# Weight chunks with the hi parts together and the lo parts behind them, at new places modulo 256 bytes

## The chip, the cores and the metric

The kernel runs on one NeuronCore of one Trainium2 chip. The metric is the device time of one execution in microseconds, the median of several runs. The profile is of one further execution.

## The reference, cut to what matters

The reference is a decoder trunk of two layers on 256 tokens of 2048 channels, in float32. Layer 0 mixes tokens with stick-breaking attention (8 heads) and a Mamba-2 SSD beside it; layer 1 with a mixture of dilated attentions (16 heads). Each layer ends with a gated ConvFFN of width 5632. Nearly all arithmetic is in large products of the activations with weight matrices:

```python
proj = hn @ w_in                      # even: 2048 x 5648, odd: 2048 x 6144
h = h + (o @ w_out)                   # 2048 x 2048 in both layers
g = causal_dwconv(hn @ w_gate, conv_w, conv_b)      # 2048 x 5632
f = (jax.nn.silu(g) * (hn @ w_up)) @ w_down         # 5632 x 2048
```

## The kernel before

Activations are kept transposed, channels on partitions and the 256 tokens along the free dimension. Each float32 operand of a large product is split into two float32r parts, hi and lo, and hi\*hi, lo\*hi and hi\*lo are summed in PSUM. An activation tile is 512 columns wide: hi parts of 256 tokens, then lo parts. Its name tells the stage: `x` holds the normed input of a layer or FFN, `act` the gated FFN activations, `o` the mixers' outputs.

A weight matrix is read in panels of 256 output channels and in chunks of `CH` = 4 tiles of 128 input channels. `prep` (lines 110 to 128) gets one chunk: a DMA brings 512 KB to `raw` (four buffers), ScalarE copies it to float32r as the hi parts (line 126), and VectorE subtracts these from `raw` for the lo parts (line 127). Both go to one tile `hl` of three buffers, in which each of the four tiles has its 256 hi columns and behind them its 256 lo columns.

`chan` (lines 142 to 158) then issues 16 matmuls for the chunk, with the weights stationary: for two tiles of 128 output channels, four matmuls of the hi weights against the whole 512-column activation tile (line 148) and four of the lo weights against its 256 hi columns (line 157). Three hi matmuls of each output tile come first, then four lo and the last hi matmul of each. `tok` (lines 160 to 182) is the other way round, used for the values of the attentions and one odd panel of 272 columns: activations are stationary, weights moving. Its line 167 streams hi and lo columns of one weight tile as 512 columns in a row, and line 174 the hi columns alone.

`products` (line 184) calls `prep` and `chan` or `tok` for one chunk after another; evictions and the attention steps are emitted between chunks. The tile framework places semaphores and lets a buffer be written again when its last reader is done.

In SBUF the pools lie one behind the other. In the built program before, the DMA scratch takes 16384 bytes per partition. The tiles of `x` (2048 bytes each), `raw` (4352 each) and `hl` (8704 each, that is 34 times 256) all start at 160 modulo 256. Behind `hl` lie the pools for evictions and norms and then the tiles of each phase: `act` at 192 modulo 256, `o` at 32 in the even layer and at 96 in the odd one. The SSD's constants `gtr` and `onesr`, stationary in lines 706 and 707, stand at 64, and its moving operand `da` at 160.

Of the kernel before, what the change touches and what calls it, by code (L numbers as in the profile page):

```python
# [21 lines left out]
FT = FF // P  # L22
CH = 4
SBH = 8
SBW = 1024
# [10 lines left out]

# columns of the parameter block
_PAR = {}
# [22 lines left out]
class Trunk:  # L61
    """The decoder trunk on activations kept transposed: channels on partitions, tokens along
    the free dimension. Every float32 operand of a large product is split exactly into two
    float32r parts of 12 significant bits each (hi + lo); hi*hi, hi*lo and lo*hi are summed in
    PSUM."""

# [22 lines left out]
    def phase(self):  # L89
        """A pool for the tiles of one mixer or FFN."""  # L90
        return self.tc.tile_pool(name=self.nm("ph"), bufs=2)
# [16 lines left out]

# [1 line left out]
    def prep(self, src, pieces=1, between=None):  # L110
        """A chunk [P, CH, ncol] of a weight matrix, split: [P, CH, (hi, lo), ncol]."""
        nc = self.nc
        ncol = src.shape[-1]
        raw = self.wraw.tile([P, CH * 272], F32, tag="raw", name=self.nm("raw"))[:, : CH * ncol]
        hl = self.whl.tile([P, CH * 544], F32R, tag="hl", name=self.nm("hl"))[:, : 2 * CH * ncol]
        raw = raw.rearrange("p (c n) -> p c n", n=ncol)
        hl = hl.rearrange("p (c t n) -> p c t n", t=2, n=ncol)
        n = CH // pieces
        parts = [slice(i * n, (i + 1) * n) for i in range(pieces)]
        for i, s in enumerate(parts):  # L120
            nc.sync.dma_start(raw[:, s], src[:, s])
            if between is not None:
                between(i)
        for s in parts:
            hi, lo = hl[:, s, 0, :], hl[:, s, 1, :]
            nc.scalar.copy(hi, raw[:, s])  # L126
            nc.vector.tensor_tensor(lo, raw[:, s], hi.bitcast(F32), ALU.subtract)  # L127
        return hl

    def log_exp(self):  # L130
        """The table set with both Ln and Exp, loaded after the last use of another."""
        with self.tc.issue_after(self.last.ins):
            self.last = self.nc.scalar.preload_act_table_set("natural_log_exp_and_others")
# [8 lines left out]
    def chan(self, accs, hl, xs, k0, start, stop):  # L142
        """Channels on partitions: acc = [hi*hi + lo*hi | hi*lo], W stationary, x moving."""
        mm = self.nc.tensor.matmul
# [15 lines left out]
    def tok(self, accs, hl, xs, k0, start, stop):  # L160
        """Tokens on partitions: acc = [hi*hi + lo*hi | hi*lo], x stationary, W moving."""
        mm = self.nc.tensor.matmul
        ncol = hl.shape[-1]
        part = lambda x, p, tt: x[:, p * T + tt * P : p * T + (tt + 1) * P]
        for tt in range(NT):
            if ncol == T:
                both = lambda k: mm(  # L167
                    accs[tt], part(xs[k0 + k], 0, tt), hl[:, k].rearrange("p t n -> p (t n)"),
                    start=start and k == 0, stop=stop and k == CH - 1,
# [14 lines left out]
    def products(self, jobs, xs, order=None, late=False):  # L184
        """Each job: (kind, panel, done); done gets the two accumulators. The first two jobs
        take their chunks in turn, which leaves time for the inputs of the last chunk. With
        late, their accumulators are read only while the third job runs (in other banks)."""
        state = [None] * len(jobs)
# [29 lines left out]
    def tick(self):  # L218
        """Lets every generator in the background emit its next step."""
        for g in list(self.bg):  # L220
            if next(g, self) is self:
                self.bg.remove(g)

    def total(self, acc):
        """hi*hi + lo*hi + hi*lo in SBUF."""
        nc = self.nc
        t = self.ev.tile([P, T], F32, tag="ev", name=self.nm("ev"))
        nc.scalar.copy(t, acc[:, T:])  # L228
        nc.vector.tensor_tensor(t, acc[:, :T], t, ALU.add)  # L229
        return t  # L230

    def padded(self, n, count):
        """Tiles [P, n + T] whose first n columns are zero."""
        out = [self.t256(f"pad{i}", 1, n + T) for i in range(count)]
# [3 lines left out]

# [1 line left out]
    def rsqrt(self, y, x, w):  # L240
        """y = 1/sqrt(x) for x > 0, [P, w]; x is overwritten."""
        nc = self.nc
# [10 lines left out]
    def stats(self, sums, inv):  # L253
        """1/rms per token of sums of squares spread over partitions: as columns
        [128 tokens, NT] and along the free dimension, on every partition."""
        nc = self.nc
# [21 lines left out]
    def token_scale(self, sums, wait, gap):  # L278
        """In the background: self.rcol and self.rbc."""
        for _ in range(wait):  # L280
# [7 lines left out]
    def square(self, sums, src, alone):  # L288
        """Adds src^2 to the list of sums, into the last one unless alone."""
        nc = self.nc  # L290
# [9 lines left out]
    def split_scaled(self, src, w):  # L300
        """The hi and lo parts of src * w (w per partition), side by side."""
        nc = self.nc
# [12 lines left out]

# [1 line left out]
    def project(self, panels, xs, normw, order=None):  # L317
        """h += (xs) @ panels; the next norm's input parts and sums of squares."""
        nc = self.nc
# [27 lines left out]

# [1 line left out]
    def ffn(self, l, xs, sums, normw):  # L349
# [40 lines left out]

# [1 line left out]
    def stick(self, q, k, v, o):  # L392
        """Two heads: q (scaled), k [128, T]; v: [128 tokens, 2 * 128] per token tile."""
        nc = self.nc
        W = 2 * (T + P)
        yield
        # columns: key tile 0 for both heads' queries, then key tile 1 for the later queries
        e = self.t256("sbe", 1, W)
# [52 lines left out]

# [1 line left out]
    def dilated(self, q, k, v, o):  # L453
        """Two heads. The softmax mixture of the branches is one softmax over the keys, each
        weighted with the number of branches that see it (its logarithm is in dbias)."""
        nc = self.nc
# [26 lines left out]
        for i in range(2):  # L483
            pt = self.psum()
            for b in range(3):
                # [q0 k0], [q1 k0], [q1 k1] -> k0: q0 q1; k1: q1
                nc.tensor.transpose(pt[:, b * P : (b + 1) * P], t3[:, i, b * P : (b + 1) * P], self.ident)  # L487
# [21 lines left out]
    def heads(self, panels, g, attend, o, v=None):  # L509
        """The products for two heads' q and k (and v), which start the attention."""  # L510
        nc = self.nc
# [33 lines left out]

# [1 line left out]
    def even(self, xs, sums, normw):  # L547
# [19 lines left out]
        def convdone(g):  # L567
            # conv channels: 8 tiles of x, 2 of B, 2 of C
            def f(accs):
# [40 lines left out]
    def decays(self, dt):  # L610
        """dt, dt * a and its sums for the SSD."""
        nc = self.nc
        v = nc.vector
        W = NT * SSH
        # dt = softplus(dt), with log1p(e) = 2 atanh(e / (2 + e)) as a series
        e = self.t256("s0", 1, W)
# [13 lines left out]
        v.scalar_tensor_tensor(dt, dt, 0.0, e, ALU.max, ALU.add)  # L630
        # dt * a, and for chunk 0 its sum over the tokens behind each one
        ea = self.t256("s3", 1, SSH)
# [16 lines left out]
    def ssd(self, dt, o):  # L649
        """Both chunks at once: y[l] = sum over s <= l of (C[l] . B[s]) exp(sum of dt * a over  # L650
        s < k <= l) xdt[s]. Blocks (chunk of s, chunk of l): 00, 01, 11."""
        nc = self.nc
        v = nc.vector
        conv = self.conv
        # x * dt, tokens on partitions
        xdt = []
        for tt in range(NT):
            for g in range(2):
# [12 lines left out]
                yield  # L671
        # masked scores [s, l] of a group
        W = 3 * P
# [15 lines left out]
        for j in range(SSH // 2):  # L689
            g = j // 4  # L690
            two = slice(2 * j, 2 * j + 2)
            # dt * a of token k, for the tokens l from k on
            parts = []
# [53 lines left out]
    def run(self, out):  # L747
# [22 lines left out]
        class Input:  # L770
            """The split tiles of x, loaded in step with the first chunks of the weights."""

# [29 lines left out]
        for step in (  # L802
# [5 lines left out]
            with self.phase() as self.ph:  # L808
                xs, sums = step(xs, sums)
        # the last norm: 1/sqrt as exp(-log/2), then a Newton step  # L810
        ps = self.psum()[:, :T]
# [19 lines left out]

# [1 line left out]
def _panels(w, groups, width=256):  # L833
    """[K, N] -> [group, chunk, partition, K tile of the chunk, column], groups of columns
    starting where `groups` says."""
    k = w.shape[0]
# [4 lines left out]
def _cols(w):  # L841
    """[..., n * 128] -> [128, ... n]"""
    return np.ascontiguousarray(w).reshape(-1, P).T
# [70 lines left out]
```

## Time and profile before

| | |
|---|---|
| median of 3 runs | 2262.81 us (2262.42 to 2263.01) |
| span of the profiled execution | 2260.8 us |
| PE busy | 2241.2 us (99%), 12880 matmuls |
| DVE busy | 1463.8 us (65%) |
| ACT busy | 1136.8 us (50%) |
| DMA | 414.09 MB, 183 GB/s on average |

The span runs from the first to the last instruction. The profiled execution's own time isn't reported apart from it; the median of the runs is 2.0 us above this span. PE is TensorE's matmuls, PEld its weight loads, DVE VectorE, ACT ScalarE. [...]

### The profile page before, as it was taken

The numbers are of one execution on the slowest core, as the hardware profiler recorded it, in microseconds if no ns is written. First come the engines' busy times: TensorE is split into PE (matmuls) and PEld (weight loads), VectorE is DVE, ScalarE is ACT, GpSimd is POOL, SyncE is SP. The second block draws the span as 40 slices with busy tenths as digits, with TensorE's granted clock in tenths as the row PEclk, the third lists the DMA queues.
The fourth block names the chain that finished last, engine by engine and source line by source line (L and its number), as shares of the span: only waits on it lengthen the run. The fifth ranks groups of instructions, "written<-read, shape, count | busy, mean of one in ns | idle before, by whom it ended". The sixth has DMA issues, their size and how long they took to land.

```text
span 2260.8 us, 33280 instructions
## 1 busy us (share of the span) xinstructions
PE 2241.2 (99%) x12880; PEld 1963.7 (87%) x12880; DVE 1463.8 (65%) x2047; ACT 1136.8 (50%) x1678; POOL 215.9 (10%) x218
## 2 busy tenths in 40 slices
PE   8999999999999999999999999999999999999997
PEld 7888888888888888888888888888888888888886
DVE  8767767766666665555565666667666666655554
ACT  6555554555555554444444454545555555544332
POOL 3013111101010110000000000111101010100000
PEclk9999999999999999999999999999999999999999
DMA  6654455555555555555555555555555555555554
GB/s 230 194 178 141 151 180 185 188 190 187 187 188 190 190 187 189 187 191 188 186 173 166 178 167 175 179 185 188 188 192 186 188 190 191 187 187 187 188 189 134
DMA packets 116110, 414.09 MB, mean 183 GB/s; under 512 B 12896, under 2 KB 15472, under 8 KB 115952
## 3 DMA queue, kind: packets, MB, share of 16 engines
q1 hardware_dynamic: 115920, 411.96, 56.1%
q8 instruction: 101, 1.65, 0.3%
q14 instruction: 57, 0.47, 0.1%
q0 software_dynamic: 32, 0.01, 0.0%
HBM read 409.82 MB, written 2.10 MB: 182 GB/s over the span
## 4 chain that ended last, share of the span: by engine, by line
PE 98%; DVE 1%; ACT 0%; DMA 0%; issue 0%; SPq 0%; POOL 0%; DVEq 0%
PE acc L148 59%; PE acc L157 30%; PE acc L167 4%; PE acc L174 2%; PE aux L465 0%; PE aux L496 0%; PE acc L179 0%; PE aux L487 0%; DMA raw<-in_wev 0%; PE aux L726 0%; DVE x L823 0%; PE aux L448 0%; PE aux L706 0%; PE aux L497 0%; PE aux L464 0%
## 5 line engine op out<-in xcount | busy, mean ns | idle before, releaser
L127 DVE TENSOR_TENSOR hl<-raw,hl 128x1024 fp32r<-128x1024 f32 (+1 forms) x779 | 959.0, 1232 | 703.4 <-ACT hl L126 702.7
L126 ACT CAST hl<-raw 128x1024 fp32r<-128x1024 f32 (+1 forms) x779 | 816.1, 1048 | 874.1 <-PE acc L148 747.8
L148 PE MATMUL acc<-x,hl 128*128 128x512 f32 x3904 | 1068.1, 393 | 0.0
L148 PEld LDWEIGHTS acc<-x,hl 128*128 128x128 f32 x3904 | 703.9, 188 | 103.6 <-issue 0.7
L157 PEld LDWEIGHTS acc<-x,hl 128*128 128x128 f32 x3904 | 600.8, 189 | 58.7
L157 PE MATMUL acc<-x,hl 128*128 128x256 f32 x3904 | 624.7, 283 | 0.0
L148 PE MATMUL acc<-act,hl 128*128 128x512 f32 x1408 | 385.5, 395 | 0.0
L148 PEld LDWEIGHTS acc<-act,hl 128*128 128x128 f32 x1408 | 251.5, 188 | 40.5
L157 PEld LDWEIGHTS acc<-act,hl 128*128 128x128 f32 x1408 | 215.2, 188 | 23.6
L157 PE MATMUL acc<-act,hl 128*128 128x256 f32 x1408 | 222.9, 280 | 0.0
L368 POOL TENSOR_TENSOR cv<-cv,rbc 128x256 f32<-128x256 f32 x88 | 95.8, 1110 | 872.5 <-ACT cv L367 872.5
L228 ACT COPY ev<-acc 128x256 f32<-128x256 f32 x244 | 90.8, 373 | 161.8 <-PE acc L148 161.8
L298 POOL TENSOR_TENSOR sum<-sum,sq 128x256 f32<-128x256 f32 x80 | 76.9, 961 | 942.0 <-ACT sq L297 933.3
L148 PE MATMUL acc<-o,hl 128*128 128x512 f32 x512 | 141.1, 396 | 0.0
L229 DVE TENSOR_TENSOR ev<-acc,ev 128x256 f32<-128x256 f32 x244 | 102.4, 421 | 20.2 <-ACT ev L228 14.2
L148 PEld LDWEIGHTS acc<-o,hl 128*128 128x128 f32 x512 | 92.1, 189 | 14.1
L167 PE MATMUL acc<-hl,x 128*128 128x512 f32 x352 | 103.2, 401 | 0.0
L157 PEld LDWEIGHTS acc<-o,hl 128*128 128x128 f32 x512 | 78.5, 188 | 8.7
L157 PE MATMUL acc<-o,hl 128*128 128x256 f32 x512 | 81.5, 281 | 0.0
L167 PEld LDWEIGHTS acc<-hl,x 128*128 128x128 f32 x352 | 61.4, 189 | 7.8 <-DVE k L527 0.3
L174 PEld LDWEIGHTS acc<-hl,x 128*128 128x128 f32 x352 | 54.0, 189 | 7.4
L174 PE MATMUL acc<-hl,x 128*128 128x256 f32 x352 | 56.4, 282 | 0.0
(166 smaller groups left out, 971.9 us busy)
## 6 DMA issues: line engine op xcount, KB each, us to landing
raw<-in_wg SPq DMA_DIRECT2D x176, 512.0 KB, 3.5
raw<-in_wu SPq DMA_DIRECT2D x176, 512.0 KB, 3.4
raw<-in_wd SPq DMA_DIRECT2D x176, 512.0 KB, 3.6
raw<-in_wod SPq DMA_DIRECT2D x96, 512.0 KB, 3.5
raw<-in_wev SPq DMA_DIRECT2D x84, 512.0 KB, 3.5
raw<-in_wevo SPq DMA_DIRECT2D x32, 512.0 KB, 4.2
raw<-in_wodo SPq DMA_DIRECT2D x32, 512.0 KB, 3.5
h<-in_x SPq DMA_DIRECT2D x16, 128.0 KB, 4.7
```

The lines of the kernel that those rows point to most:

```text
L126: nc.scalar.copy(hi, raw[:, s])
L127: nc.vector.tensor_tensor(lo, raw[:, s], hi.bitcast(F32), ALU.subtract)
L148: mm(accs[nt], hl[:, k, 0, nt * P : (nt + 1) * P], xs[k0 + k], start=start and k == 0, stop=stop and k == CH - 1,)
L157: mm(accs[nt][:, :T], hl[:, k, 1, nt * P : (nt + 1) * P], xs[k0 + k][:, :T], start=False, stop=False)
L167: both = lambda k: mm(accs[tt], part(xs[k0 + k], 0, tt), hl[:, k].rearrange("p t n -> p (t n)"), start=start and k == 0, stop=stop and k = ...
L174: mm(accs[tt][:, :T], part(xs[k0 + k], 1, tt), hl[:, k, 0, :], start=False, stop=False)
L228: nc.scalar.copy(t, acc[:, T:])
L229: nc.vector.tensor_tensor(t, acc[:, :T], t, ALU.add)
L298: nc.gpsimd.tensor_tensor(sums[-1], sums[-1], sq, ALU.add)
L368: nc.gpsimd.tensor_tensor(c, c, self.rbc, ALU.mult)
```

## The change

The tile `hl` becomes two rows, one of all hi parts of the chunk and one of all lo parts. Each row is 1088 columns and 8 more (`LOW`), 4384 bytes, which is 32 more than a multiple of 256; the two rows make 8768 bytes, 64 more than a multiple of 256. The view that `prep` returns still has the dimensions tile, part and column, so `chan` is unchanged; the moving operand in line 167 of `tok` and its accumulator get two dimensions. The scratch for software DMAs is set to 8192 bytes. Comments are dropped, which changes nothing that runs.

```diff
 CH = 4
+LOW = 8
...
         raw = self.wraw.tile([P, CH * 272], F32, tag="raw", name=self.nm("raw"))[:, : CH * ncol]
-        hl = self.whl.tile([P, CH * 544], F32R, tag="hl", name=self.nm("hl"))[:, : 2 * CH * ncol]
+        hl = self.whl.tile([P, 2, CH * 272 + LOW], F32R, tag="hl", name=self.nm("hl"))
         raw = raw.rearrange("p (c n) -> p c n", n=ncol)
-        hl = hl.rearrange("p (c t n) -> p c t n", t=2, n=ncol)
+
+        hl = hl[:, :, : CH * ncol].rearrange("p t (c n) -> p c t n", n=ncol)
...
                 both = lambda k: mm(
-                    accs[tt], part(xs[k0 + k], 0, tt), hl[:, k].rearrange("p t n -> p (t n)"),
+                    accs[tt].rearrange("p (t n) -> p t n", t=2), part(xs[k0 + k], 0, tt), hl[:, k],
...
-    nc = _bacc.Bacc("TRN2", target_bir_lowering=False, num_devices=1)
+    nc = _bacc.Bacc("TRN2", target_bir_lowering=False, num_devices=1, dynamic_dma_scratch_size=8192)
```

## Rows read from the trace of the kernel before

**Rows 1.** The page: the span, busy time of PE with its share and instructions, the granted TensorE clock in 40 slices, and the chain that ended last by engine and by line.

```profile
span 2260.8 us, 33280 instructions
PE 2241.2 (99%) x12880; PEld 1963.7 (87%) x12880; DVE 1463.8 (65%) x2047; ACT 1136.8 (50%) x1678; POOL 215.9 (10%) x218
...
PEclk9999999999999999999999999999999999999999
...
PE 98%; DVE 1%; ACT 0%; DMA 0%; issue 0%; SPq 0%; POOL 0%; DVEq 0%
PE acc L148 59%; PE acc L157 30%; PE acc L167 4%; PE acc L174 2%; PE aux L465 0%; PE aux L496 0%; PE acc L179 0%; PE aux L487 0%; DMA raw<-in_wev 0%; PE aux L726 0%; DVE x L823 0%; PE aux L448 0%; PE aux L706 0%; PE aux L497 0%; PE aux L464 0%
```

**Rows 2.** The page's costliest groups: busy us, mean ns of one, then idle time of the engine before them and what ended it.

```profile
L127 DVE TENSOR_TENSOR hl<-raw,hl 128x1024 fp32r<-128x1024 f32 (+1 forms) x779 | 959.0, 1232 | 703.4 <-ACT hl L126 702.7
L126 ACT CAST hl<-raw 128x1024 fp32r<-128x1024 f32 (+1 forms) x779 | 816.1, 1048 | 874.1 <-PE acc L148 747.8
L148 PE MATMUL acc<-x,hl 128*128 128x512 f32 x3904 | 1068.1, 393 | 0.0
...
L157 PE MATMUL acc<-x,hl 128*128 128x256 f32 x3904 | 624.7, 283 | 0.0
L148 PE MATMUL acc<-act,hl 128*128 128x512 f32 x1408 | 385.5, 395 | 0.0
...
L148 PE MATMUL acc<-o,hl 128*128 128x512 f32 x512 | 141.1, 396 | 0.0
...
L167 PE MATMUL acc<-hl,x 128*128 128x512 f32 x352 | 103.2, 401 | 0.0
```

**Rows 3.** PE's matmuls in order of time with `x` moving (first FFN), equal ones merged: start, us from the first start to the last end, count. The first and the last row of a repetition are four chunks apart, 64 matmuls.

```profile
531.10 1.77 PE L148 MATMUL acc<-x,hl 128*128 128x512 f32 x7
532.70 0.64 PE L157 MATMUL acc<-x,hl 128*128 128x256 f32 x4
533.17 0.40 PE L148 MATMUL acc<-x,hl 128*128 128x512 f32 x1
...
542.27 0.63 PE L148 MATMUL acc<-x,hl 128*128 128x512 f32 x2
```

**Rows 4.** The same with `act` moving (first FFN's last product); the rows are three chunks apart.

```profile
1009.38 1.80 PE L148 MATMUL acc<-act,hl 128*128 128x512 f32 x7
...
1017.80 1.80 PE L148 MATMUL acc<-act,hl 128*128 128x512 f32 x7
```

**Rows 5.** The same with `o` moving (even layer's output product); each row starts the next chunk.

```profile
362.45 1.79 PE L148 MATMUL acc<-o,hl 128*128 128x512 f32 x7
...
365.26 1.79 PE L148 MATMUL acc<-o,hl 128*128 128x512 f32 x7
...
368.09 1.79 PE L148 MATMUL acc<-o,hl 128*128 128x512 f32 x7
...
370.89 1.79 PE L148 MATMUL acc<-o,hl 128*128 128x512 f32 x7
```

**Rows 6.** Busy time of each engine in two stretches: length, then PE, PEld, DVE, ACT and POOL with counts, granted clock, DMA share and GB/s. The first has four chunks with `x`, the second four with `act`.

```profile
531.10:542.27 11.17, 11.17 (x67) 9.84 (x65) 7.85 (x13) 6.30 (x10) 2.21 (x2) 1.00 0.60 187
1009.38:1020.61 11.23, 11.23 (x67) 9.77 (x65) 4.90 (x4) 4.22 (x4) 0.00 (x0) 1.00 0.57 188
```

**Rows 7.** Groups of matmuls within windows, columns as in rows 2: from 531.3 to 1000 us, from 1000 to 1140 us, then two windows of some ten ns inside one chunk with `x` (at 532.0 and 532.72).

```profile
L148 PE MATMUL acc<-x,hl 128*128 128x512 f32 x985 | 266.5, 392 | 0.0
L157 PE MATMUL acc<-x,hl 128*128 128x256 f32 x984 | 157.5, 283 | 0.0
...
L148 PE MATMUL acc<-act,hl 128*128 128x512 f32 x346 | 94.9, 395 | 0.0
L157 PE MATMUL acc<-act,hl 128*128 128x256 f32 x352 | 55.7, 280 | 0.0
...
L148 PE MATMUL acc<-x,hl 128*128 128x512 f32 x2 | 0.6, 389 | 0.0
L157 PE MATMUL acc<-x,hl 128*128 128x256 f32 x1 | 0.3, 277 | 0.0
```

**Rows 8.** Smaller groups of matmuls over the span, columns as in rows 2. Lines 464 and 465 are plain float32 products (each in two passes), lines 706 and 707 float32r ones of the SSD.

```profile
L465 PE MATMUL aux<-k,q 128*128 128x256 f32 x32 | 9.6, 380 | 0.0
...
L464 PE MATMUL aux<-k,q 128*128 128x128 f32 x32 | 6.1, 274 | 0.0
...
L706 PE MATMUL aux<-da,gtr 128*128 128x512 f32 x16 | 6.0, 395 | 0.0
...
L707 PE MATMUL aux<-da,onesr 128*128 128x256 f32 x16 | 4.5, 279 | 0.0
```

**Rows 9.** PE's matmuls, and below them PE's weight loads (PEld), in order of time around 150.5 us, where a product of the SSD follows a chunk.

```profile
150.32 0.40 PE L148 MATMUL acc<-x,hl 128*128 128x512 f32 x1
150.65 0.66 PE L726 MATMUL aux<-ex,ssd 128*64 128x256 f32 x4
...
150.20 0.19 PEld L148 LDWEIGHTS acc<-x,hl 128*128 128x128 f32 x1
150.65 0.20 PEld L726 LDWEIGHTS aux<-ex,ssd 128*64 128x64 f32 x4 [0.26 <-issue]
```

**Rows 10.** The page's group of line 228, and its DMA queue of software descriptors (packets, MB, share of 16 engines).

```profile
q0 software_dynamic: 32, 0.01, 0.0%
...
L228 ACT COPY ev<-acc 128x256 f32<-128x256 f32 x244 | 90.8, 373 | 161.8 <-PE acc L148 161.8
```

## The prediction

> **What bounds the kernel now.** I read the page first, then the groups of matmuls, then single chunks in order of time. [...]
>
> A chunk of `chan` is eight matmuls of 512 columns (hi parts stationary) and eight of 256 (lo parts stationary). With the normed input `x` moving, four chunks take 542.27 - 531.10 = 11.17 us, 2.793 each [rows 3]. With `act` moving three take 1017.80 - 1009.38 = 8.42 us, 2.807 each [rows 4]. In the even layer's output projection, with `o` moving, three follow each other at 2.81, 2.83 and 2.80 us, 2.813 on average [rows 5]. There are 488, 176 and 64 such chunks (3904, 1408 and 512 matmuls by eight) and 44 full `tok` chunks (352 by eight) [rows 2], together nearly the whole span.
>
> **What lengthens a matmul.** A record of a matmul runs on past the start of the next one. In [rows 3] seven 512-column matmuls cover 1.77 us and the next starts 1.60 after the first, a tail of 0.17; for `act` it is much the same. I use 163 ns. Then 392 ns (mean of 985 with `x` moving) is a spacing of about 229, and 395 (with `act`) is 232 [rows 7]. A plain float32 pass over 256 columns lasts 380 ns, a spacing of 217 [rows 8]. Nearly the same time for half the columns: it reads its moving operand at half the rate. So the float32r stream loses 12 to 15 ns in each 512 columns, and there is something to gain if addresses are the cause.
>
> Who takes it? Not the other engines: over four `x` chunks VectorE is busy 7.85 of 11.17 us and GpSimd 2.21, over four `act` chunks 4.90 and none [rows 6], yet the busier stretch has the shorter chunks. Nor, mostly, the weight load beside it: the matmul that starts at 150.32 has no weight load beside its stream after its own, since the next one starts at 150.65; its record is 0.40 long, like the 0.40 of the one at 533.17, which has one [rows 3, 9].
>
> [...]
>
> **The change, part by part.** First the addresses. In the built program `x`, `raw` and all three `hl` buffers start at 160 modulo 256; `act` stands at 192, `o` at 32 (even) and 96 (odd). Each hi and lo piece begins at a multiple of 512 bytes inside its buffer. So the distance from moving operand to the weights is 0 for `x`, 224 for `act`, 128 and 64 for `o`. After the change the hi parts stand at 160, 224 and 32 in the three buffers and the lo parts at 192, 0 and 64. `x` stays; what lies behind `hl` moves by 3 x 64 = 192, so `act` goes to 128 and `o` to 224 and 32. The distances with `x` become 0, 64, 128 (hi) and 32, 96, 160 (lo).
>
> The trace has seen several of these. At 224 the records are 395 and 280 ns [rows 7]; at 128 and 64, in the output projections, the chunks average 2.813 us or a little less [rows 5]. The weights `gtr` and `onesr` of the SSD's sums stand at 64 with the moving operand at 160, a distance of 160: 395 and 279 ns [rows 8]. None comes near 380. The one thing that distance 0 seems to give is a run of 512-column matmuls at 389 ns, 226 of spacing [rows 7], which other stages hold less often.
>
> *hi parts with `x`.* Two of three buffers leave distance 0. I charge them the 3 ns by which 395 exceeds 392: 8 x 3 x 2/3 = 16 ns a chunk, x 488 = +7.8 us. Bounds: 0 if distance doesn't matter, +11.7 if all three lose it.
>
> *lo parts with `x`.* They leave distance 0 too. A chunk with `act` is 2.807 - 2.793 = 14 ns longer in all although its hi part is 8 x 3 = 24 ns longer, so its lo part is 10 ns shorter (283 against 280 ns points the same way). At 32, 96 and 160 I expect that: -10 x 488 = -4.9 us. Bounds: 0, and -11.7 at the 3 ns by which the records differ.
>
> *`act` and `o`.* They go from one set of distances to another; the nearest rows are 2.807 and 2.813 a chunk, so +6 ns x 176 x half = +0.5 us, bounds -1 to +1.
>
> *`tok`.* The 512 moving columns are now two pieces of 256, 4384 bytes apart. The nearest row is line 707, whose moving operand is two pieces of 128: 279 ns, and a 256-column one in a single piece (line 157 with `act`) takes 280 [rows 7, 8]. So 0; at 4 ns for each of 352 it would be +1.4 us, and I see no gain.
>
> *Cast and subtraction.* They now write 1024 elements in a row instead of four runs of 256. A 256-element copy takes 373 ns and the 1024-element cast 1048 [rows 2, 10], 0.88 ns an element in the difference, which leaves no visible price for breaks between runs; I take 0. Whatever it is lies under PE: ScalarE sits idle 874 us before the casts, almost all of it waiting for PE. If that cover were gone, 10 ns on 779 casts would be 8 us.
>
> *Scratch of 8192 bytes.* It shifts everything by a multiple of 256, and only the 32 packets of one software queue use it [rows 10]: 0.
>
> The sum is 7.8 - 4.9 + 0.5 = +3.4 us. The profiled execution has a span of 2260.8; with the 2.0 us around it that the median of 2262.81 implies, the base is 2262.8, and the sum gives 2266.2. I predict 2266 us.
>
> **The rivals.** A measurement of this kernel tells no change from one within 0.2%, 4.5 us.
>
> *Slower.* The short runs of 389 ns depend on all weights standing at the same distance, and the lo parts gain nothing. Then `x` chunks take 2.813 as with `o` (+20 ns x 488 = +9.8) and `act` chunks +6 ns (+1.1): 2274 us. For it speaks that the stage with equal distance 0 is the fastest of the three; against it, that the 256-column records are the longest there. It decides as soon as the lo parts give back less than 3.8 us.
>
> *Faster, in part.* What lengthens the matmuls is after all two reads of TensorE in one slice of 256 bytes, and with hi and lo in different slices most spacings fall to the shortest seen: 389 - 163 = 226 and 277 - 163 = 114 [rows 7], 8 x 226 + 8 x 114 = 2.72 us a chunk. That saves 73, 87 and 93 ns in 488, 176 and 64 chunks, 36 + 15 + 6 = 57 us: 2206. Half of it is 2234. Against it stands the matmul at 150.32, and that all distances seen give 392 to 396.
>
> *Faster, in full.* Spacings like float32's, 217 and (from 274 ns) 111: 2.62 us a chunk, saving 173, 187 and 193 ns: 84 + 33 + 12 = 129 us, 2134. No float32r row at full clock comes there.
>
> **How the numbers follow.** I give the forecast 0.35 (its own range 2259 to 2267), slower 0.30, faster in part 0.31, in full 0.04. These are the chances of same, slower and faster (0.35). The range runs from 2222, which leaves out the full case and the deepest third of the part, to 2276, just over the slower rival with the price of `tok`.
>
> **What would show it.** If I am right, the mean of line 148 with `x` rises from 393 towards 395 and that of line 157 falls from 283 towards 280; `x` chunks no longer repeat one length but go through three, one for each buffer. Records of 512 columns below 389 ns in numbers would prove me wrong towards faster; means of 396 and 283 together towards slower. If lines 126 and 127 change by more than 20 ns, or PE starts waiting for VectorE, the layout has touched what I put at nothing.

## The result, and the profile after

The changed kernel takes 2269.12 us (median of 8 runs, 2268.84 to 2269.47) against 2262.99 for the kernel before beside it (8 runs): a ratio of 1.0027, 95% interval 1.0018 to 1.0036. It is slower by 6.1 us, and the spans of the two profiled executions stand 6.5 us apart (2260.8 and 2267.3).

The page after, its first part, chain and largest groups; the lines of `chan` are now 150 (hi, 148 before) and 159 (lo, 157 before):

```profile
span 2267.3 us, 33280 instructions
...
PE 2248.7 (99%) x12880; PEld 1961.2 (87%) x12880; DVE 1463.5 (65%) x2047; ACT 1135.8 (50%) x1678; POOL 215.3 (9%) x218
...
PEclk9999999999999999999999999999999999999999
...
PE 98%; DVE 1%; ACT 0%; DMA 0%; SPq 0%; issue 0%; POOL 0%; DVEq 0%
...
L129 DVE TENSOR_TENSOR hl<-raw,hl 128x1024 fp32r<-128x1024 f32 (+1 forms) x779 | 959.5, 1232 | 707.3 <-ACT hl L128 706.7
L128 ACT CAST hl<-raw 128x1024 fp32r<-128x1024 f32 (+1 forms) x779 | 814.6, 1046 | 879.5 <-PE acc L150 751.3
L150 PE MATMUL acc<-x,hl 128*128 128x512 f32 x3904 | 1077.7, 395 | 0.0
...
L159 PE MATMUL acc<-x,hl 128*128 128x256 f32 x3904 | 621.5, 281 | 0.0
L150 PE MATMUL acc<-act,hl 128*128 128x512 f32 x1408 | 386.0, 396 | 0.0
...
L150 PE MATMUL acc<-o,hl 128*128 128x512 f32 x512 | 140.4, 395 | 0.0
L169 PE MATMUL acc<-hl,x 128*128 128x512 f32 x352 | 103.5, 402 | 0.0
```

PE is still 98% of the chain, at the same granted clock (0.998 in both executions), and still waits for nobody: the cast and the subtraction have their durations of before within 2 ns [rows 2], and more idle time in front of them. What moved is the records of the hi matmuls with `x`, 393 to 395 ns, and of the lo ones, 283 to 281.

The chunks with `x` after, in order of time (start, us, count). The rows are one chunk apart: the seven matmuls are the last one of a chunk and the first six of the next.

```profile
695.50 1.79 PE L150 MATMUL acc<-x,hl 128*128 128x512 f32 x7
698.30 1.81 PE L150 MATMUL acc<-x,hl 128*128 128x512 f32 x7
701.13 1.79 PE L150 MATMUL acc<-x,hl 128*128 128x512 f32 x7
703.93 1.77 PE L150 MATMUL acc<-x,hl 128*128 128x512 f32 x7
706.72 1.79 PE L150 MATMUL acc<-x,hl 128*128 128x512 f32 x7
709.53 1.78 PE L150 MATMUL acc<-x,hl 128*128 128x512 f32 x7
712.34 1.79 PE L150 MATMUL acc<-x,hl 128*128 128x512 f32 x7
```

Before, 404 of 487 chunks took 2.793 or 2.794 us [rows 3]; most of the others are longer. Now the lengths change from chunk to chunk, 2.80, 2.83, 2.80, 2.79, 2.81 and 2.81, and repeat after six: 16.84 / 6 = 2.807 on average. Fourteen ns more in each of 488 chunks are 6.8 us.

Records overlap, in [rows 3] by 0.17 us, so I also added up all spacings from one matmul's start to the next one's in both traces, over all whole chunks:

| | before, us | after, us | difference |
|---|---|---|---|
| hi matmuls with `x` (487 chunks) | 900.6 | 910.7 | +10.1 |
| lo matmuls with `x` | 464.7 | 461.9 | -2.8 |
| chunks with `act` (176) | 493.9 | 494.0 | 0.0 |
| chunks with `o` (64) | 180.1 | 179.4 | -0.8 |
| `tok`, full chunks | 126.2 | 126.4 | +0.2 |

That adds up to +6.7 us, against 6.5 between the spans.

### The profile page after: what moved, and what is told of

It reads as the page before. It is cut to its first block, busy times and chain, and to the rows that moved or that the text cites. A ratio compares the mean times of both kernels' runs of the same rounds, so it can differ in the third digit from the quotient of the medians.

```text
span 2267.3 us, 33280 instructions
## 1 busy us (share of the span) xinstructions
PE 2248.7 (99%) x12880; PEld 1961.2 (87%) x12880; DVE 1463.5 (65%) x2047; ACT 1135.8 (50%) x1678; POOL 215.3 (9%) x218
## 4 chain that ended last, share of the span: by engine, by line
PE 98%; DVE 1%; ACT 0%; DMA 0%; SPq 0%; issue 0%; POOL 0%; DVEq 0%
PE acc L150 59%; PE acc L159 30%; PE acc L169 4%; PE acc L176 2%; PE aux L467 0%; PE aux L498 0%; PE acc L181 0%; DMA raw<-in_wev 0%; PE aux L489 0%; PE aux L728 0%; DVE x L825 0%; PE aux L450 0%; PE aux L708 0%; PE aux L499 0%; PE aux L466 0%; PE aux L406 0%
```

## The experiments

Theory 1 was that of the prediction: the distance modulo 256 from the moving operand to the weights sets a matmul's spacing. The rivals: storing the parts together, or the 32 bytes by themselves, or the place of one operand alone. All these kernels compute the whole reference, and where a ratio is given it is to the kernel before on the same chip.

**Storing together alone** (also with the smaller scratch and the two-piece operand of `tok`):

```diff
-LOW = 8
+LOW = 0
```

> The hi parts of a chunk stored together and the lo parts behind them, with nothing added between them: hi and lo parts and all three buffers begin at 160 modulo 256 again, as before the change. Theory 1 (the distance modulo 256 between the moving operand and the stationary parts sets a matmul's spacing): as before, 2263 us, an x chunk at 2.793 us, means of 393 and 283 ns. Rival (the storing together does it, by whatever way: writes in one run, hi parts 1024 bytes apart instead of 2048): 2269 us, means of 395 and 281 ns with x.

Measured: 2263.06 us, ratio 0.9999 (0.9990 to 1.0009). The chunks with `x`:

```profile
531.90 1.77 PE L150 MATMUL acc<-x,hl 128*128 128x512 f32 x7
534.70 1.77 PE L150 MATMUL acc<-x,hl 128*128 128x512 f32 x7
537.49 1.77 PE L150 MATMUL acc<-x,hl 128*128 128x512 f32 x7
540.28 1.77 PE L150 MATMUL acc<-x,hl 128*128 128x512 f32 x7
```

8.38 / 3 = 2.793 again, and the means are 393 and 283 ns. Everything in the change but the two offsets costs nothing that shows. The lo parts now begin 4352 bytes behind the hi parts, 17 times 256, where it was 1024, 4 times 256: a shift of the lo parts by a whole multiple of 256 changed nothing.

**The stride of the buffers alone:**

```diff
-LOW = 8
+LOW = 0
-        hl = self.whl.tile([P, 2, CH * 272 + LOW], F32R, tag="hl", name=self.nm("hl"))
+        hl = self.whl.tile([P, 2 * (CH * 272) + 16], F32R, tag="hl", name=self.nm("hl"))
+        hl = hl[:, : 2 * CH * 272].rearrange("p (t n) -> p t n", t=2)
```

> Hi parts together, lo parts at the same place modulo 256 as their hi parts, but the three buffers 64 bytes apart modulo 256: with x the distances are 0, 64 and 128 for hi and lo alike; act and o lie where the change puts them. Theory 1: x chunks of two of the three buffers lengthen to 2.81 or 2.82 us and nothing is given back by the lo parts: 2269 to 2272 us, hi mean 395 ns. Rival (the stride is harmless, the 32 bytes between hi and lo do it): 2263 us.

Measured: 2267.13 us, ratio 1.0018 (1.0008 to 1.0027), 4.0 us slower. The group's rows:

```profile
L151 PE MATMUL acc<-x,hl 128*128 128x512 f32 x3904 | 1076.9, 395 | 0.0
L160 PE MATMUL acc<-x,hl 128*128 128x256 f32 x3904 | 618.9, 281 | 0.0
```

The hi mean is the forecast one. The time lies under the forecast range because the lo parts did give something back: with the three buffers at 0, 64 and 128 their spacings add up to 458.8 us, 5.9 less than before, while the hi parts' rise by 9.6. The `x` chunks have medians of 2.802, 2.796 and 2.809 us in turn, so only one of three comes near the 2.81 that I forecast for two. `act` costs 2.0 more, `o` 1.1 less.

**The 32 bytes alone**, all buffers alike:

```diff
-        hl = self.whl.tile([P, 2, CH * 272 + LOW], F32R, tag="hl", name=self.nm("hl"))
+        hl = self.whl.tile([P, 2 * (CH * 272 + LOW) + 48], F32R, tag="hl", name=self.nm("hl"))
+        hl = hl[:, : 2 * (CH * 272 + LOW)].rearrange("p (t n) -> p t n", t=2)
```

> Hi parts together, lo parts 32 bytes further modulo 256, but all three buffers at the same place modulo 256: with x the distances are 0 (hi) and 32 (lo) in every chunk; act and o lie as before the change. Theory 1: the hi mean stays at 393 ns, the lo mean falls from 283 to 280 ns, an x chunk takes 2.78 to 2.79 us, 2257 to 2260 us in all. Rival (the 32 bytes are what costs): 2267 us or more, hi mean 395 ns or more.

Measured: 2264.68 us, ratio 1.0007 (0.9998 to 1.0016). A miss for my gain of 3 to 6 us, and no 2267 either. Its rows:

```profile
L151 PE MATMUL acc<-x,hl 128*128 128x512 f32 x3904 | 1070.7, 394 | 0.0
...
L160 PE MATMUL acc<-x,hl 128*128 128x256 f32 x3904 | 623.2, 281 | 0.0
```

The records of the lo matmuls are 2 ns shorter, as I forecast nearly, and yet their spacings add up to 464.7 us, the sum of before to the tenth. The record's mean is no measure of the spacing here: the profile models the ends of matmuls. The hi part rises by 2.4 us, although its own distance is still 0. Most `x` chunks alternate between 2.814 and 2.779 us from first matmul to first matmul, 2.797 on average, a little above the 2.793 of distance 0. The rows, which start at a chunk's last matmul, show 2.82 and 2.78:

```profile
801.09 1.78 PE L151 MATMUL acc<-x,hl 128*128 128x512 f32 x7
803.91 1.77 PE L151 MATMUL acc<-x,hl 128*128 128x512 f32 x7
806.69 1.78 PE L151 MATMUL acc<-x,hl 128*128 128x512 f32 x7
```

**The weights left alone, `x` moved by 64 bytes** (distance 192):

```diff
+        pool("pa", 1).tile([P, 16], F32, name="pa")
         self.xp = pool("xp", KT)
+        pool("pb", 1).tile([P, 48], F32, name="pb")
```

> The weights exactly as before the change; alone the x tiles lie 64 bytes further (224 modulo 256 instead of 160), so that the distance with x is 192 in place of 0. Theory 1: the x chunks lose their length of 2.793 us and take 2.80 to 2.82, 2266 to 2274 us, with act and o chunks unchanged at 2.807 and 2.813. Rival (the place or the layout of the weights alone matters, not the distance): 2263 us, x chunks at 2.793.

Measured: 2249.98 us, ratio 0.9943 (0.9926 to 0.9959). The lengths with `x` did change, but downwards, 13 us faster. The chunks:

```profile
799.64 1.78 PE L150 MATMUL acc<-x,hl 128*128 128x512 f32 x7
802.41 1.78 PE L150 MATMUL acc<-x,hl 128*128 128x512 f32 x7
805.17 1.78 PE L150 MATMUL acc<-x,hl 128*128 128x512 f32 x7
807.94 1.78 PE L150 MATMUL acc<-x,hl 128*128 128x512 f32 x7
```

8.30 / 3 = 2.767, against 2.793. Neither forecast came out. Moving `x` alone does change the length, as Theory 1 says, unless it is the place of `x` itself; my idea that distance 0 is the best one falls.

**The same distance with `x` in its old place:** the 192 bytes behind `x` alone (the second of the two added lines, none before `x`).

> The kernel before with x where it was (160 modulo 256) and raw, hl and all behind them 192 bytes further, so that the weights stand at 96, act at 128, o at 224 and 32. The distance with x is 192, as in the run that moved x; with act and o it is 224, 128 and 64 as before. Theory 1 (the distance sets the spacing): x chunks at 2.767 us like in that run, act 2.807, o 2.81: 2250 us. Rival (the place of x alone made that run faster): x chunks at 2.793, 2263 us.

Measured: 2250.01 us, ratio 0.9943 (0.9927 to 0.9959), chunks with `x` as above:

```profile
531.11 1.78 PE L149 MATMUL acc<-x,hl 128*128 128x512 f32 x7
533.88 1.78 PE L149 MATMUL acc<-x,hl 128*128 128x512 f32 x7
536.65 1.78 PE L149 MATMUL acc<-x,hl 128*128 128x512 f32 x7
539.41 1.78 PE L149 MATMUL acc<-x,hl 128*128 128x512 f32 x7
```

It is the distance, not the place of either operand.

**Distance 192 everywhere.** To the edit that moved `x` come a 32-byte tile before `act`, one of 128 bytes before the odd layer's `o`, one of 192 before the even layer's:

```diff
         gpad = self.padded(2, 3)
+        self.t256("apd", 1, 8)
...
+        self.t256("opd", 1, 32)
         o = [self.big("o", KT) for _ in range(KT)]
```

> The kernel before with x, act and both o tiles at 224 modulo 256, so that the distance to the weights (160) is 192 in every chunk. Theory 1: every chunk takes 2.767 us; act saves 40 ns x 176 = 7.0 us and o 46 ns x 64 = 2.9 us beyond the run that moved x alone: 2240 us. Rival (what happened with x is a matter of that stage): act chunks at 2.807, 2250 us.

Measured: 2240.29 us (4 runs, 2240.09 to 2240.81), ratio 0.9900 (0.9882 to 0.9918). The forecast of 2240 came out. Chunks with `act`, then with `o` of the even layer, then the matmul before a product of the SSD, as in rows 9:

```profile
1009.21 1.78 PE L150 MATMUL acc<-act,hl 128*128 128x512 f32 x7
1011.97 1.78 PE L150 MATMUL acc<-act,hl 128*128 128x512 f32 x7
...
360.88 1.78 PE L150 MATMUL acc<-o,hl 128*128 128x512 f32 x7
363.64 1.78 PE L150 MATMUL acc<-o,hl 128*128 128x512 f32 x7
...
150.40 0.40 PE L150 MATMUL acc<-x,hl 128*128 128x512 f32 x1
150.72 0.66 PE L731 MATMUL aux<-ex,ssd 128*64 128x256 f32 x4
```

Both stages, 2.807 and 2.81 before [rows 4, 5], now take 2.76 to 2.77, the length with `x`. This kernel beats both, by 22.6 us the one before and by 28.8 the changed one.

One more rival can be settled from these traces: ScalarE and VectorE write the next buffer of `hl`, at the same place modulo 256, while PE reads, and the distance might work through them. But when the last weights have been split, PE still has chunks to do. Here are one chunk beside a cast and a subtraction and the next one without, at distance 192 and then in the kernel before at 224 (length, then PE, PEld, DVE, ACT and POOL, granted clock, DMA share and GB/s):

```profile
2217.07:2219.84 2.77, 2.77 (x18) 2.43 (x16) 1.23 (x1) 1.05 (x1) 0.00 (x0) 1.00 0.00 0
2219.84:2222.61 2.77, 2.77 (x18) 2.43 (x17) 0.00 (x0) 0.00 (x0) 0.00 (x0) 1.00 0.03 6
...
2238.67:2241.48 2.81, 2.81 (x17) 2.44 (x16) 1.23 (x1) 1.05 (x1) 0.00 (x0) 1.00 0.00 0
2241.48:2244.29 2.81, 2.81 (x18) 2.44 (x16) 0.00 (x0) 0.00 (x0) 0.00 (x0) 1.00 0.02 6
```

With VectorE, ScalarE and GpSimd idle and the DMAs at 2 or 3%, the chunk keeps its length within 1 ns in both kernels. So the length doesn't come from the other engines' writes.

**Other distances**, one run each, tiles moved by such pads. First, hi and lo parts alike:

> The kernel before with its tiles moved so that hi and lo parts stand at distances not seen with every buffer so far: 160 with x, 32 with act, 96 with o of the even layer, 160 with o of the odd one. Theory 1: one chunk length for one distance, so x and the odd layer's o agree within 10 ns; lengths between 2.76 and 2.82 us. If place in SBUF matters beyond the distance, x and o at 160 differ by more.

Measured: 2279.02 us. With `x` at 160:

```profile
532.28 1.79 PE L150 MATMUL acc<-x,hl 128*128 128x512 f32 x7
535.11 1.79 PE L150 MATMUL acc<-x,hl 128*128 128x512 f32 x7
537.94 1.79 PE L150 MATMUL acc<-x,hl 128*128 128x512 f32 x7
```

2.83 a chunk, the slowest seen, and the odd layer's `o` at the same distance agrees with it (medians of 2.827 and 2.827). One value lies beyond the range I gave.

Then, weights 16 bytes further in their buffers, for distances halfway:

> The kernel before with the weights 16 bytes further inside their buffers (176 modulo 256) and the tiles moved, so that the distances are 208 with x, 176 with act, 240 with o of the even layer and 16 with o of the odd one: halves of 32 bytes. Theory 1: chunk lengths between those of the neighbours: about 2.79 with x (192 gives 2.767, 224 2.807), 2.80 with act (160 gives 2.827), 2.80 with both o. If only the 32-byte slice counts, each equals one of its neighbours.

Measured: 2262.68 us; chunks of 2.800 us at 208, 2.793 at 176, 2.767 at 240 and 2.820 at 16. At 208 and 176 the length lies between the neighbours', at 16 and 240 it does not: neither of my two forms holds. `raw`, which stood at the same place modulo 256 as the weights in the runs at 160 and 192, stayed at 192 from `x` here, and the chunk with `x` took 2.800 and not 2.767: what counts is the distance to the weights that PE reads and not to `raw`. At 240, with `o` of the even layer:

```profile
362.02 1.76 PE L150 MATMUL acc<-o,hl 128*128 128x512 f32 x7
364.79 1.76 PE L150 MATMUL acc<-o,hl 128*128 128x512 f32 x7
```

With what came before, median length of a chunk by the distance of hi and lo alike (16, 176, 208 and 240 from this run alone; 16, 64, 96, 128 and 240 from 32 chunks with `o` each; at 128 lengths of 2.820, 2.803 and 2.811 take turns):

| distance | us | distance | us |
|---|---|---|---|
| 0 | 2.793 | 160 | 2.827 |
| 16 | 2.820 | 176 | 2.793 |
| 32 | 2.807 | 192 | 2.767 |
| 64 | 2.813 | 208 | 2.800 |
| 96 | 2.807 | 224 | 2.807 |
| 128 | 2.811 | 240 | 2.767 |

**Hi and lo at different distances:** the 32-byte offset, and one of 64 bytes (`LOW = 16`), with all buffers alike.

> Hi parts together, lo parts 32 bytes further, all buffers at 160 modulo 256, tiles moved so that the distances of hi and lo are 192 and 224 with x, 96 and 128 with act, 160 and 192 with o of the even layer, 32 and 64 with o of the odd one. Theory 1: with x the hi part is as short as at 192 (about 1.84 us in a steady chunk) but the lo part loses its 27 ns: chunks of 2.78 to 2.80 us. Rival (hi and lo at different places is what helps): below 2.767.

> Hi parts together, lo parts 64 bytes further modulo 256, all buffers alike; tiles moved so that the distances of hi and lo are 192 and 0 with x, 128 and 192 with act, 160 and 224 with o of the even layer, 32 and 96 with o of the odd one. Theory 1 with each weight load counting by itself: an x chunk lies between 2.767 (192 alone) and 2.793 (0 alone), an act chunk between 2.767 and 2.811. Rival (what counts is that hi and lo parts stand alike): both above 2.80.

Measured: 2251.92 and 2252.46 us. With 192 and 224 a chunk with `x` takes 2.773 us, shorter than I forecast but not below 2.767. Added up over the run its lo matmuls take 6.3 us more than in the run that moved `x`, and its hi matmuls, at the same distance, 4.0 less. With 192 and 0 it takes 2.773 too, between the 2.767 and 2.793 of the two distances alone, and `act` with 128 and 192 takes 2.800, between 2.767 and 2.811:

```profile
1013.74 1.78 PE L153 MATMUL acc<-act,hl 128*128 128x512 f32 x7
1016.54 1.78 PE L153 MATMUL acc<-act,hl 128*128 128x512 f32 x7
1019.34 1.78 PE L153 MATMUL acc<-act,hl 128*128 128x512 f32 x7
```

It doesn't have to be the same distance for both. But that each load brings a price of its own, as Theory 1 had it here, isn't shown. In the first of these runs `act` with 96 and 128 takes 2.800, less than at either distance alone (2.807 and 2.811), and so does the odd layer's `o` with 32 and 64 (2.807 and 2.813):

```profile
1013.29 1.79 PE L153 MATMUL acc<-act,hl 128*128 128x512 f32 x7
1016.09 1.79 PE L153 MATMUL acc<-act,hl 128*128 128x512 f32 x7
```

The combination of distances sets the length of a chunk, and it can't be added up from the lengths that each gives alone.

## Why the prediction was right or wrong, point by point

The time, 2269.1, lies in the range, 3 us above the 2266 forecast, and outside the likeliest case's own range. The range was 54 us wide, so holding a change of 6 says little for the sum. By the bound of 0.2% the kernel is slower, the case that I gave 0.30.

*The bound.* I added up spacings of matmuls and nothing else, and rightly: PE is 98% of the chain before [rows 1] and after, and the other engines' work stayed hidden.

*Hi parts with `x`.* Right in kind and nearly in size: +7.8 forecast, +10.1 found, inside the bounds of 0 and +11.7. The stride alone makes 9.6 of it. That the size came so near is in part luck: the 3 ns came from records, at a distance of 224 that `x` doesn't have after the change.

*Lo parts with `x`.* This is the step that was mis-sized: -4.9 forecast, -2.8 found. I took what `act` shows at 224 for distances of 32, 96 and 160. The run with 32 alone shows that 32 beside hi parts at 0 gives the lo parts nothing (464.7 us before and in it). Which buffer gave the 2.8 us isn't shown for certain: taken by every third chunk the lo sums change by -1.5, -0.2 and -1.1 us, which are the buffers at 32, 96 and 160 if the program's first chunk has the first buffer. Either way a price per distance, carried from stage to stage, was the wrong tool. I also leaned on records, 283 and 280 ns, and the same run shows records shortened by 2 ns at unchanged spacings. With -2.8 and the +10.1 of the hi parts the sum goes past the bound of 0.2%.

*`act` and `o`.* +0.5 forecast, 0.0 and -0.8 found; single buffers went both ways, the odd layer's `o` from 2.813 us a chunk to medians of 2.821, 2.806 and 2.780. *`tok`, cast, scratch:* zero forecast, +0.2 us and zero found.

*The slower rival* (2274) had its condition met, lo parts that give back less than 3.8 us, but `x` chunks reached 2.807 in the stretch shown and not 2.813; over all of them the rise is 15 ns a chunk, not 20.

*The faster rivals.* The change did not bring them, but the argument I set against them is refuted. I held that distances seen so far all gave 392 to 396 ns and that the weight load beside a stream mattered little. I had seen no stage at 192 throughout, and there a chunk loses 26 ns against distance 0 and 40 against 224. The partial rival's times, from 2206 to the 2258 where the bound of 0.2% begins, hold the 2240 that the right distance gives, but not for its reason: 128, as far from 0 as can be, takes 2.811.

*What stays open.* The runs show that the distances set the spacings, not by what mechanism. At distance 192 the matmul that starts at 150.40 has no next load beside it (line 731 follows 0.32 later) and is still 0.40 long, like the one at 150.32 before [rows 9]. That would say that not all of what lies above the 217 ns of a float32 pass over 256 columns [rows 8] comes from the load beside the stream, but it rests on two records whose ends are modelled, as did my argument in the prediction, and isn't shown.

*The marks I set.* The means went to 395 and 281 as I wrote, yet the time left its range: they were too coarse. The chunks go through six lengths, not three: each buffer takes two in turn.

## What to carry to other kernels

In this kernel, which runs float32r matmuls back to back at a granted clock of 0.998, the distance modulo 256 bytes between the moving tile and the weights is worth up to 2% of a chunk (2.767 to 2.827 us), and a pad of 32 to 224 bytes in a pool sets it. In a kernel like it, try several distances in the kernel itself, and keep the same good one for every buffer and every stage. An offset that spreads buffers over several distances got something in between, and here it gave up one of the better ones. Compare spacings from start to start; means of overlapping records can move without them.

## What the runs showed of the hardware that I had not expected

The dependence is fine and not smooth: steps of 16 bytes take a chunk from 2.767 (240) over 2.793 (0) to 2.820 (16), and from 2.827 (160) over 2.793 (176) to 2.767 (192). Those in steps of 16 come from one run, with the weights moved. At 192 the length is the same to the ns whether `x` or the weights are moved, and with 192 everywhere it is the same with `x`, where VectorE is busy 7.10 of 11.20 us, and with `act`, where it is busy 4.94 of 11.07.

The lengths come in steps, too. In all twelve traces and all four stages (`x`, `act`, `o` of either layer) the most frequent length of six chunks in a row is a whole multiple of 6.67 ns to within a ns: 16.600 us at 192 is 2490 of them, 16.760 at 0 is 2514, 16.840 at 224 is 2526, 16.960 at 160 is 2544. Where the step comes from isn't shown.
